# Delta-rule layer: the inverses' scratch X1 is laid into the substitution's tiles Lb and Tb

## The chip, the cores and the metric

The kernel runs on one core of one Trainium2 chip. The metric is the device time of one launch in microseconds (us), and the median over runs is compared. The engines are called as in the profile: PE (TensorE, matrix products; PEld are its weight loads), DVE (VectorE), ACT (ScalarE), POOL (GpSimd) and SP (SyncE, which issues most of the loads from DRAM). A "q" behind a name means that engine's queue of instructions.

## What is computed

A decoder trunk of four residual layers on x of 256 tokens by 1024 channels, in float32: a pooling layer, a gated delta-rule layer, a latent-attention layer, and a pooling layer again. The change lies in the delta-rule layer alone. The core of its reference:

```python
q, k, v = jnp.split(silu(causal_depthwise_conv(qkv, conv_w)), ...)
...
L = jnp.where(strict, jnp.einsum('bhnid,bhnjd->bhnij', k_beta, k) * decay, 0.0)
A = jnp.eye(C) + L
rhs = jnp.concatenate([v_beta, k_beta * jnp.exp(g)[..., None]], axis=-1)
sol = lax.linalg.triangular_solve(A, rhs, left_side=True, lower=True)
u_ps, w_cd = sol[..., :dv], sol[..., dv:]
attn = jnp.where(causal, jnp.einsum('bhnid,bhnjd->bhnij', q, k) * decay, 0.0)

def step(state, xs):            # over the chunks
    v_new = u_c - w_c @ state
    o = (q_c * exp(g_c)) @ state + a_c @ v_new
    state = state * exp(g_last) + k_dec.T @ v_new
```

There are 8 heads with keys of 128 and values of 256 channels. The triangular system is what the changed tiles serve: the kernel inverts the unit lower triangular matrices instead of solving for each right side.

## The kernel before, in words

The 256 tokens are two tiles of 128 (t = 0, 1), and the kernel takes chunks of 128 tokens, so there are 2 × 8 = 16 matrices of 128 × 128 to invert. Weights come in units of 512 KB through three buffers raw (issued by SP, L104); each is split into a rounded part whi (ACT, L117) and a remainder wlo (DVE, L119; a few on POOL), and three products of the parts stand for one float32 product (L127 to L129, and L168).

In `gdn_layer` one list sets the order of the steps on each engine's list:

```python
order = "g0 k0 d a0 g1 k1 a1 s q0 v0 v1 v2 q1 V3 i c3 g2 u0 u1 g3".split()
```

Here g are gate projections, k keys, a the lower matrices LT, s the substitution, q the queries (two halves of four heads), v values (V3 and c3 are the two halves of v3), i the inverses, u the new values. A scheduler then merges these lists, gives tiles their places in the fast memory and adds the waits. All big tiles (4 KB in each of the 128 partitions) share one pool, `s4`, which has as many slots as the program needs; a tile that takes over a slot waits until the last instruction on the slot's former tile is done.

- **Substitution (s).** The four diagonal blocks of 32 × 32 of each of the 16 matrices go from LT to DRAM (d_l) and come back as Lb, 64 partitions of one block each. POOL inverts them row by row: 31 pairs of a product pr (L728, reads Lb and Tb) and a subtraction from Tb (L732). Then Tb goes to DRAM (d_t, L735), and four transfers (L739) bring the blocks into the diagonal of the tile T. All five are on POOL's queue.
- **Queries (q1).** A projection, a short convolution (ACT L634, DVE L637 into cv), SiLU into the tile kqT (ACT, L671), then transposes (PE, L677) and products with the keys (PE, L690). POOL multiplies the last tokens' queries into Gb (L760) and works out their norms (L761 to L765); these are held back behind the substitution.
- **Inverses (i).** POOL clears a part of each scratch tile X1 (L810; the profile writes X1 and its like as X), DVE transposes T into U (L811), and two steps of doubling follow: products of LT with T (PE, L820) go masked into X1 (DVE, L822), products of X1 with U (PE, L826) correct U, and so on up to L847. L820 reads columns 0–31 and 64–95 of each head of T.
- **Gate 2 (g2).** Its result gsg (ACT, L557) is a big tile, too.

Of the kernel before, what the change touches and what calls it, by code (L numbers as in the profile page):

```python
# [16 lines left out]
P = 128  # L17
D = 1024
S = 256
NT = S // P  # L20
# [22 lines left out]
def trunk(ctx: ExitStack, tc: tile.TileContext, x, positions, norm_g, pool_w_in, pool_w_grp,  # L43
# [26 lines left out]
    def big(name, *dims, dt=F32):  # L70
        return s4.tile([P, *dims], dt, tag="s4", name=name)
# [4 lines left out]
    def workb(name, *dims):  # L76
        return wb.tile([P, *dims], F32, tag="wb", name=name)

    def small(name, *dims, bufs=2):
        return sm.tile([P, *dims], F32, tag=name, name=name, bufs=bufs)  # L80

    def bank(pool, name):
        return pool.tile([P, CW], F32, tag=name, name=name)
# [452 lines left out]
    def gdn_layer(i, j, hT):  # L536
        H = GDN_H
        M = NT * H
# [101 lines left out]


        Q, B = 4, 32
        Tb = big("Tb", B, B)[:M * Q]
        nc.gpsimd.memset(Tb, 0.0)
        nc.gpsimd.memset(Tb.rearrange("m r c -> m (r c)")[:, ::B + 1], 1.0)
        Ts = big("T", NT, H, P)
# [67 lines left out]
        def substitution():  # L714

            d_l = dram.tile([M * Q, B * B], F32, name="d_l")
            lv = d_l.rearrange("(t m d) (r c) -> t d r m c", t=NT, d=Q, r=B)
            for t in range(NT):
                for d in range(Q):
                    nc.sync.dma_start(out=lv[t, d],  # L720
                                      in_=LT[t][d * B:(d + 1) * B, :, d * B:(d + 1) * B])
            Lb = big("Lb", B, B)[:M * Q]
            nc.sync.dma_start(out=Lb, in_=d_l.rearrange("m (r c) -> m r c", r=B))
            pr = small("pr", 256, bufs=1)[:M * Q]
            for r in range(B - 1):
                n, c = B - 1 - r, r + 1
                pv = pr[:, :n * c].rearrange("m (a b) -> m a b", a=n)
                nc.gpsimd.tensor_tensor(out=pv, op=ALU.mult,  # L728
                                        in0=Lb[:, r, r + 1:, None].to_broadcast([M * Q, n, c]),
                                        in1=Tb[:, r:r + 1, :c].to_broadcast([M * Q, n, c]))  # L730
                tv = Tb[:, r + 1:, :c]
                mark["blocks"] = nc.gpsimd.tensor_tensor(out=tv, in0=tv, in1=pv,  # L732
                                                         op=ALU.subtract).ins
            d_t = dram.tile([M * Q, B * B], F32, name="d_t")
            nc.gpsimd.dma_start(out=d_t.rearrange("m (r c) -> m r c", r=B), in_=Tb)  # L735
            tv = d_t.rearrange("(m d) (r c) -> d r m c", d=Q, r=B)
            for d in range(Q):
                dd = slice(d * B, (d + 1) * B)
                nc.gpsimd.dma_start(out=Ts[dd, :, :, dd].rearrange("p t h c -> p (t h) c"),  # L739
                                    in_=tv[d])  # L740
            nc.vector.reciprocal(rki, rk)
            nc.vector.tensor_tensor(out=kds, in0=rk[:, 0, :], in1=DT[0][:, :, P - 1],
                                    op=ALU.mult)
            nc.vector.tensor_scalar(neG, eG[:, 1, :], -1.0, None, ALU.mult)
            nc.gpsimd.tensor_tensor(out=ktok, in0=ktok, op=ALU.mult,
                                    in1=kds[:, :, None].to_broadcast([P, H, P]))
# [54 lines left out]
        def inverses():  # L801

            U.extend(big("U", H, P) for _ in range(NT))
            X1 = [big("X1", H, P) for _ in range(NT)]
            for t in range(NT):
                nc.gpsimd.memset(X1[t][:, :, 32:64], 0.0)  # L810
                nc.vector.transpose(U[t].rearrange("p m c -> p (m c)"),  # L811
                                    T[t].rearrange("p m c -> p (m c)"))

            def blocks(a, x):
                return a.rearrange("p m (a b c) -> p m a b c", a=2, b=2)[:, :, :, x]

            def pairs(t):
                ps = bank(aux, "aux").rearrange("p (m a c) -> p m a c", m=H, a=2)
                for h in range(H):
                    nc.tensor.matmul(ps[:, h], lhsT=LT[t][:, h], rhs=blocks(T[t], 0)[:, h],  # L820
                                     start=True, stop=True)
                nc.vector.tensor_tensor(out=blocks(X1[t], 0), in0=ps, op=ALU.mult,  # L822
                                        in1=m32[:, None].to_broadcast([P, H, 2, 32]))
                ps = bank(aux, "aux").rearrange("p (m a c) -> p m a c", m=H, a=2)
                for h in range(H):
                    nc.tensor.matmul(ps[:96, h], lhsT=X1[t][:, h, :96], rhs=blocks(U[t], 1)[:, h],  # L826
                                     start=True, stop=True)
                u = blocks(U[t], 1)[:96]
                nc.vector.tensor_tensor(out=u, in0=u, in1=ps[:96], op=ALU.subtract)

            def whole(t):
                ps = bank(aux, "aux").rearrange("p (m c) -> p m c", m=H)
                for h in range(H):
                    nc.tensor.transpose(ps[:64, h], U[t][:64, h, :64], ident[:64, :64])
                nc.scalar.copy(T[t][:64, :, :64], ps[:64])
                ps = bank(aux, "aux").rearrange("p (m c) -> p m c", m=H)
                for h in range(H):
                    nc.tensor.matmul(ps[:, h], lhsT=LT[t][:64, h], rhs=T[t][:64, h, :64],
                                     start=True, stop=True)
                X = workb("X", H, 64)  # L840
                nc.vector.tensor_copy(X[64:], ps[64:])
                ps = bank(aux, "aux").rearrange("p (m c) -> p m c", m=H)
                for h in range(H):
                    nc.tensor.matmul(ps[:64, h], lhsT=X[64:, h], rhs=U[t][64:, h, 64:],
                                     start=True, stop=True)
                u = U[t][:64, :, 64:]
                nc.vector.tensor_tensor(out=u, in0=u, in1=ps[:64], op=ALU.subtract)  # L847

            for stage in (pairs, whole):
                for t in range(NT):  # L850
                    stage(t)

        def news(hf):
# [3 lines left out]
            for b in range(2):  # L857
# [6 lines left out]
                for c in range(2):  # L864
# [4 lines left out]
        steps = {"g": gate, "k": keys, "a": lower, "q": queries, "v": values, "u": news, "V": values_in,  # L869
                 "c": values_done}  # L870
        once = {"s": substitution, "d": decays, "i": inverses}
        for name in order:
            if name == "i":

                with later(mark["strip"], mark["dve"]):
                    inverses()
            elif name in once:
                once[name]()
            else:
                steps[name[0]](int(name[1]))  # L880
# [124 lines left out]
    def mla_layer(i, j, hT):  # L1005
# [203 lines left out]
        return layer_out(mla_w_out[j], yT, units(POOL_W // P), i)  # L1209

    layers = (pool_layer, gdn_layer, mla_layer)
    setups = [gdn_setup, mla_setup][:max(0, depth - 1)]
    first = cols_of(pool_w_in[0], POOL_W + (len(WINDOWS) - 1) * CW)
# [58 lines left out]
```

## Time and profile before

| | |
|---|---|
| median of 3 runs | 859.29 us (856.95 to 861.53) |
| profiled execution | 860.12 us, its span from first to last instruction 858.3 us |
| busy in the span | PE 836.9, DVE 594.2, ACT 490.2, POOL 155.2 us |
| mean granted clock of PE | 0.988 of full speed |
| HBM | read 137.79 MB, 162 GB/s over the span |

The kernel is bound by PE nearly everywhere. A row of the timeline reads: start (us from the span's start), duration, engine, line, operation, written tile <- read tiles, shapes, and in brackets how long the engine stood idle before it and what ended that. The delta-rule layer's substitution, second query half and inverses lie between 255 and 355 us.

### The profile page before, as it was taken

How to read it: one execution, taken by the hardware profiler on the slowest of the kernel's cores; microseconds unless marked ns; L12 is line 12 of the kernel's file. 1: busy time of each engine (PE TensorE's matmuls, PEld its weight loads, DVE VectorE, ACT ScalarE, POOL GpSimd, SP SyncE). 2: the span in 40 equal slices, each digit the busy share in tenths (PEclk: the TensorE clock that was granted, in tenths of full speed). 3: DMA queues.
4: the chain of work that ended last, by engine and by line, in shares of the span. 5: the costliest groups of instructions: out<-in, count | busy, mean ns of one | idle time of the engine just before them, and what ended most of it. 6: DMA issues, size and time to landing. Idle time of an engine off the chain costs nothing.

```text
span 858.3 us, 16132 instructions
## 1 busy us (share of the span) xinstructions
PE 836.9 (98%) x5967; PEld 778.9 (91%) x5967; DVE 594.2 (69%) x1140; ACT 490.2 (57%) x1007; POOL 155.2 (18%) x295
## 2 busy tenths in 40 slices
PE   6999999999999989999999999999999999999996
PEld 5999998988999988788979998999989989999986
DVE  4689866556988976355577659678767668867852
ACT  5566564467855744355465654566555475555642
POOL 4000000233237980022212002000000210000012
PEclk8999999999999999899999999999999999999999
DMA  6766666646655554123547676743552546556551
GB/s 196 245 190 185 179 194 198 194 138 198 193 141 168 171 149 131 66 67 106 173 139 217 198 171 172 195 127 97 172 163 82 175 148 209 182 179 196 190 201 50
DMA packets 109239, 140.42 MB, mean 164 GB/s; under 512 B 21228, under 2 KB 51112, under 8 KB 109160
## 3 DMA queue, kind: packets, MB, share of 16 engines
q1 hardware_dynamic: 106800, 137.65, 53.1%
q0 software_dynamic: 528, 1.58, 0.7%
q8 instruction: 47, 0.77, 0.4%
q10 hardware_dynamic: 1832, 0.16, 0.2%
q14 instruction: 32, 0.26, 0.1%
HBM read 137.79 MB, written 1.58 MB: 162 GB/s over the span
## 4 chain that ended last, share of the span: by engine, by line
PE 82%; POOL 7%; DVE 5%; DMA 3%; issue 2%; ACT 1%; SPq 0%; POOLq 0%; ACTq 0%; DVEq 0%
PE acc L168 33%; PE acc L128 11%; PE acc L127 11%; PE acc L129 11%; POOL Tb L732 3%; POOL pr L728 2%; PE aux L127 2%; PE aux L128 2%; PE aux L129 2%; DVE wlo L119 1%; DMA gain<-in_norm_g_dram 1%; DVE cv L637 1%; DVE h L304 1%; PE aux L861 1%; DMA Gb<-d_g 1%
## 5 line engine op out<-in xcount | busy, mean ns | idle before, releaser
L119 DVE TENSOR_TENSOR wlo<-raw,whi 128x512 fp32r<-128x512 f32 (+1 forms) x493 | 342.5, 717 | 162.6 <-ACT whi L117 155.4
L117 ACT CAST whi<-raw 128x512 fp32r<-128x512 f32 (+1 forms) x508 | 301.8, 617 | 256.7 <-PE acc L168 100.4
L127 PE MATMUL acc<-hTh,whi 128*128 128x256 f32 x832 | 234.3, 282 | 1.2 <-DVE vc L637 1.2
L128 PE MATMUL acc<-hTl,whi 128*128 128x256 f32 x832 | 235.0, 283 | 0.0
L129 PE MATMUL acc<-hTh,wlo 128*128 128x256 f32 x832 | 233.8, 281 | 0.0
L127 PEld LDWEIGHTS acc<-hTh,whi 128*128 128x128 f32 x832 | 156.9, 189 | 1.8 <-DVE vc L637 1.4
L128 PEld LDWEIGHTS acc<-hTl,whi 128*128 128x128 f32 x832 | 156.9, 189 | 0.4
L129 PEld LDWEIGHTS acc<-hTh,wlo 128*128 128x128 f32 x832 | 156.8, 189 | 0.2
L168 PE MATMUL acc<-wlo,yTh 128*128 128x256 f32 (+1 forms) x384 | 116.5, 319 | 0.0
L168 PE MATMUL acc<-whi,yTh 128*128 128x256 f32 (+1 forms) x384 | 116.4, 323 | 0.0
L168 PE MATMUL acc<-whi,yTl 128*128 128x256 f32 (+1 forms) x384 | 92.7, 322 | 0.0
L168 PEld LDWEIGHTS acc<-wlo,yTh 128*128 128x128 f32 x384 | 72.1, 188 | 5.1
L168 PEld LDWEIGHTS acc<-whi,yTh 128*128 128x128 f32 x384 | 71.7, 188 | 5.2
L168 PEld LDWEIGHTS acc<-whi,yTl 128*128 128x128 f32 x384 | 63.2, 188 | 5.5
L292 POOL TENSOR_TENSOR hg<-x,gain 128x256 f32<-128x256 f32 x18 | 14.9, 834 | 259.1 <-DVE x L354 257.4
L168 PE MATMUL acc<-wlo,hTh 128*128 128x512 f32 (+1 forms) x144 | 56.3, 396 | 0.4 <-DVE wlo L119 0.2
L168 PE MATMUL acc<-whi,hTh 128*128 128x512 f32 (+1 forms) x144 | 55.6, 394 | 0.7 <-ACT hTh L196 0.7
L168 PE MATMUL acc<-whi,hTl 128*128 128x512 f32 (+1 forms) x144 | 45.7, 389 | 0.0
L435 POOL COPY win<-u 128x4 f32<-128x4 f32 x8 | 2.8, 355 | 177.2 <-ACT u L429 177.2
L168 PEld LDWEIGHTS acc<-whi,hTh 128*128 128x128 f32 x144 | 27.5, 191 | 6.8 <-ACT hTh L196 1.7
L168 PEld LDWEIGHTS acc<-wlo,hTh 128*128 128x128 f32 x144 | 27.3, 190 | 6.8 <-DVE wlo L119 1.7
L168 PEld LDWEIGHTS acc<-whi,hTl 128*128 128x128 f32 x144 | 26.8, 190 | 5.5
(339 smaller groups left out, 1444.5 us busy)
## 6 DMA issues: line engine op xcount, KB each, us to landing
raw<-in_pool_w_in_dram SPq DMA_DIRECT2D x60, 512.0 KB, 4.5
raw<-in_gdn_w_in_dram SPq DMA_DIRECT2D x48, 512.0 KB, 3.9
raw<-in_pool_w_out_dram SPq DMA_DIRECT2D x32, 512.0 KB, 4.2
raw<-in_mla_w_in_dram SPq DMA_DIRECT2D x24, 512.0 KB, 4.6
raw<-in_mla_w_uq_dram SPq DMA_DIRECT2D x36, 256.0 KB, 3.4
raw<-in_pool_w_grp_dram SPq DMA_DIRECT2D x16, 512.0 KB, 4.1
raw<-in_gdn_w_out_dram SPq DMA_DIRECT2D x16, 512.0 KB, 3.7
raw<-in_mla_w_ukv_dram SPq DMA_DIRECT2D x32, 256.0 KB, 3.3
```

Source lines behind the costliest of these rows:

```text
L117: a = nc.scalar.copy(hi, v)
L119: b = e.tensor_tensor(out=lo, in0=v, in1=hi.bitcast(F32), op=ALU.subtract)
L127: nc.tensor.matmul(o, lhsT=lhs[0], rhs=rhs[0], start=start, stop=False)
L128: nc.tensor.matmul(o, lhsT=lhs[0], rhs=rhs[1], start=False, stop=False)
L129: return nc.tensor.matmul(o, lhsT=lhs[1], rhs=rhs[0], start=False, stop=stop)
L168: nc.tensor.matmul(o, lhsT=act(k, t * P, P)[x], rhs=parts[j][z][:, sl], start=k == first and x == z == 0, stop=k == last and x == 1)
L292: nc.gpsimd.tensor_tensor(out=self.early[t, a], in0=xs[t][:, sl], in1=self.g[:, sl], op=ALU.mult)
L304: nc.vector.scalar_tensor_tensor(out=h[:, cut:], in0=xs[t][:, sl], scalar=r[:, 0:1], in1=self.g[:, sl], op0=ALU.mult, op1=ALU.mult)
L637: nc.vector.scalar_tensor_tensor(out=o[:, d:], in0=ps[:, :S - d], scalar=tp(3 - d, c), in1=o[:, d:], op0=ALU.mult, op1=ALU.add)
L728: nc.gpsimd.tensor_tensor(out=pv, op=ALU.mult, in0=Lb[:, r, r + 1:, None].to_broadcast([M * Q, n, c]), in1=Tb[:, r:r + 1, :c].to_broadcast ...
L732: mark["blocks"] = nc.gpsimd.tensor_tensor(out=tv, in0=tv, in1=pv, op=ALU.subtract).ins
L861: nc.tensor.matmul(ps[:, c], lhsT=U[0][:, h, :], rhs=vR[h // 2][:, 0, c * DV:(c + 1) * DV], start=True, stop=True)
```

## The change

X1 is no longer a tile of its own. The substitution keeps its two tiles Lb and Tb whole (they use 64 of 128 partitions), and the inverses take them as scratch: X1[0] is Lb, X1[1] is Tb.

```diff
-        Tb = big("Tb", B, B)[:M * Q]
+        Tb_ = big("Tb", B, B)
+        Tb = Tb_[:M * Q]
+        free = []
...
-            Lb = big("Lb", B, B)[:M * Q]
+            Lb_ = big("Lb", B, B)
+            Lb = Lb_[:M * Q]
+            free.extend((Lb_, Tb_))
...
-            X1 = [big("X1", H, P) for _ in range(NT)]
+            X1 = [a.rearrange("p (h a) c -> p h (a c)", h=H) for a in free]
```

The pool has 29 slots before and after. Before, kqT of q1 took Lb's slot as soon as the substitution was done with it, and gsg of g2 took it after that; X1[0] lay in a slot that nothing had used, and X1[1] took Tb's. Now Lb and Tb keep their slots until the inverses are done with X1; kqT of q1 takes the slot that X1[0] had, and gsg takes Lb's when X1[0] is done. No other big tile is moved, and no instruction is added or removed. In the changed kernel's lists the lines stand 2 to 5 higher (L671 is L673, L728 is L732, L732 is L736, L739 is L743, L810 is L815, L820 is L825).

On ACT, at kqT of q1 (cv are the convolved queries; whi the splits between), the list before:

```order
L791 ACTIVATE vR_3807<-tp_3835,rki_2523 128x256
L634 ACTIVATE cv_3994<-acc_3843,tap_648 128x256
L117 CAST whi_4336<-raw_4329 128x512 [waits PE_49]
L671 ACTIVATE kqT_3980<-cv_3981 128x256 [waits DVE_49,Activation_49,Pool_49]
L117 CAST whi_4354<-raw_4351 128x512 [waits DMAHW0_49,PE_49]
L671 ACTIVATE kqT_3980<-cv_3982 128x256 [waits DVE_49,Activation_49]
```

And now:

```order
L795 ACTIVATE vR_3807<-tp_3835,rki_2523 128x256
L634 ACTIVATE cv_3994<-acc_3843,tap_648 128x256
L117 CAST whi_4334<-raw_4327 128x512 [waits PE_49]
L673 ACTIVATE kqT_3980<-cv_3981 128x256 [waits DVE_49,Activation_49]
L117 CAST whi_4352<-raw_4349 128x512 [waits DMAHW0_49,PE_49]
L673 ACTIVATE kqT_3980<-cv_3982 128x256 [waits DVE_49,Activation_49]
```

The order is the same; the first kqT instruction no longer waits for POOL.

On POOL, at the end of the substitution, the list before:

```order
L732 TENSOR_TENSOR Tb<-Tb,pr 64x2x30
L728 TENSOR_TENSOR pr<-Lb,Tb 64x31
L732 TENSOR_TENSOR Tb<-Tb,pr 64x31
L760 TENSOR_TENSOR Gb<-Gb,kqT 128x512
L761 TENSOR_SCALAR rq_2525<-ssq 128x2x4
L735 DMA d_t<-Tb 64x1024
L810 MEMSET X_4184 128x8x32
L659 TENSOR_TENSOR rq<-rq_2525,halves 128x2x4
L119 TENSOR_TENSOR wlo<-raw,whi 128x512
L739 DMA T<-d_t 32x16x32 x4
L764 TENSOR_TENSOR rq_2525<-rq 128x2x4
L760 TENSOR_TENSOR Gb<-Gb,kqT 128x512
```

And now:

```order
L736 TENSOR_TENSOR Tb<-Tb,pr 64x2x30
L815 MEMSET Lb 128x8x32
L732 TENSOR_TENSOR pr<-Lb,Tb 64x31
L736 TENSOR_TENSOR Tb<-Tb,pr 64x31
L764 TENSOR_TENSOR Gb<-Gb,kqT 128x512
L765 TENSOR_SCALAR rq_2525<-ssq 128x2x4
L739 DMA d_t<-Tb 64x1024
L661 TENSOR_TENSOR rq<-rq_2525,halves 128x2x4
L119 TENSOR_TENSOR wlo<-raw,whi 128x512
L743 DMA T<-d_t 32x16x32 x4
L768 TENSOR_TENSOR rq_2525<-rq 128x2x4
L815 MEMSET Tb 128x8x32
```

The memset of X1[0] (now in Lb) moved from behind d_t to ahead of the last pair of the substitution; that of X1[1] (now in Tb) moved up from behind the split wlo that follows the second Gb product, to ahead of that product. The lists of PE, DVE, ACT and SP hold the same instructions in the same order as before, with X1's name changed.

## The prediction

> **What bounds the kernel now.** I began with the page: the span, the busy times and the chain that ended last.
>
> ```profile
> span 858.3 us, 16132 instructions
> PE 836.9 (98%) x5967; PEld 778.9 (91%) x5967; DVE 594.2 (69%) x1140; ACT 490.2 (57%) x1007; POOL 155.2 (18%) x295
> PE 82%; POOL 7%; DVE 5%; DMA 3%; issue 2%; ACT 1%; SPq 0%; POOLq 0%; ACTq 0%; DVEq 0%
> ```
>
> TensorE (PE) is busy 98% of the span, so a change gains only what it takes out of PE's idle time or its slow clock. What stands out is POOL, busy 18% of the span, with 7% of the chain. The timeline around the change shows where POOL enters; I read ACT, POOL, PE and DVE there in turn.
>
> ```profile
> 301.17 0.66 ACT L117 CAST whi<-raw 128x512 fp32r<-128x512 f32 x1
> 305.29 0.42 ACT L671 ACTIVATE kqT<-cv 128x256 f32<-128x256 f32 x1 [3.46 <-POOL pr L728]
> 305.02 0.23 POOL L728 TENSOR_TENSOR pr<-Lb,Tb 64x31 f32<-64x31 f32 x1
> 303.07 0.28 PE L129 MATMUL acc<-hTh,wlo 128*128 128x256 f32 x1
> 305.76 0.69 PE L677 MATMUL tp<-ident,kqT 128*128 128x128 f32 x2 [2.41 <-ACT kqT L671]
> 306.25 1.12 DVE L119 TENSOR_TENSOR wlo<-raw,whi 128x512 fp32r<-128x512 f32 x1 [2.25 <-ACT whi L117]
> 300.14 2.80 DVE L637 SCALAR_TENSOR_TENSOR cv<-acc,tap,cv 128x254 f32<-128x254 f32 x6
> ```
>
> ACT is free at 301.83 and stands 3.46 us, until the last product that reads Lb (305.02 + 0.23) is done: the second half of the queries, kqT, lies in Lb's slot. PE, done at 303.35, stands 2.41 us for the transposes of kqT. DVE stands 2.25 us for a split queued on ACT behind kqT. The convolution that feeds kqT was not late: six steps take 2.80 us, and the first two of them complete the first tile by about 301.1.
>
> PE pays for this stall twice. The windows view, cut where the granted clock (PEclk) changes, shows it:
>
> ```profile
> core 0: us, PE busy (x) PEld busy (x) DVE busy (x) ACT busy (x) POOL busy (x), PEclk, DMA share, GB/s
> 298.49:301.90 3.41, 3.41 (x32) 3.41 (x31) 3.34 (x7) 3.34 (x9) 3.02 (x6) 1.00 0.86 224
> ...
> 301.90:305.31 3.41, 1.45 (x13) 1.25 (x11) 2.06 (x5) 0.02 (x1) 2.81 (x8) 1.00 0.40 105
> 305.31:308.72 3.41, 2.96 (x14) 2.96 (x15) 2.47 (x5) 3.12 (x7) 3.24 (x6) 0.50 0.38 136
> ```
>
> After a window in which PE was idle 1.96 of 3.41 us, the next 3.41 us ran at clock 0.50. With 2.96 us of work in it, that cost half, 1.48 us. So the stall delays PE by 2.41 + 1.48 = 3.89 us.
>
> Whether that is a delay of the kernel is decided at the next place where PE meets POOL: the inverses' first product (L820), which reads T, the tile that POOL's substitution fills through DRAM. I followed POOL there.
>
> ```profile
> 305.33 0.25 POOL L732 TENSOR_TENSOR Tb<-Tb,pr 64x31 f32<-64x31 f32 x1
> 305.54 1.27 POOL L760 TENSOR_TENSOR Gb<-Gb,kqT 128x512 f32<-128x512 f32 x1
> 306.90 0.52 POOL L761 TENSOR_SCALAR rq<-ssq 128x8 f32<-128x8 f32 x1
> 307.48 0.67 POOL L735 DMA_DIRECT2D d_t<-Tb  x1
> 308.14 0.34 POOL L810 MEMSET X<- 128x256 f32 x1
> 308.42 1.85 POOL L659 TENSOR_TENSOR rq<-rq,halves 128x8 f32<-128x8 f32 x1
> 310.25 1.27 POOL L119 TENSOR_TENSOR wlo<-raw,whi 128x512 fp32r<-128x512 f32 x1
> 311.48 1.39 POOL L739 DMA_DIRECT2D T<-d_t  x2
> 312.86 1.29 POOL L739 DMA_DIRECT2D T<-d_t  x2
> ...
> DMA to landing us min/median/max: 3.0/3.0/3.0
> ...
> T<-d_t POOLq DMA_DIRECT2D x1, 64.0 KB, 5.0
> ...
> T<-d_t POOLq DMA_DIRECT2D x1, 64.0 KB, 5.9
> ...
> SPq L104 <- POOL wlo L119: 4.1, 1, 4.1
> ```
>
> No row here has an idle bracket: POOL works without a pause from the substitution to the four transfers into T. The lines below the timeline are the times from issue to landing of d_t, of the first and of the second T transfer, and the wait of SP's queue, whose next weight load stood 4.1 us for that last POOL split. The first T transfer lands at 311.48 + 5.0 = 316.5. The second starts at about 312.2 (half of 1.39 us on) and lands at about 318.1. L820 reads columns 0–31 and 64–95 of each head, which two of the four transfers fill.
>
> ```profile
> 317.79 0.19 PEld L168 LDWEIGHTS acc<-whi,hTh 128*128 128x128 f32 x1
> 318.21 1.86 PEld L820 LDWEIGHTS aux<-T,LT 128*128 128x128 f32 x16 [0.24 <-issue]
> 318.75 1.25 DVE L811 STREAM_TRANSPOSE U<-T 128x1024 f32<-128x1024 f32 x1 [1.91 <-DMA T<-d_t]
> ```
>
> PE loads L820's weights at 318.21, 0.24 us after it was ready and 0.1 us after the second landing; DVE, which needs all four, starts at 318.75. So two paths meet at 318.1: PE's own, with the 3.89 us of stall in it, and POOL's substitution with its two trips through DRAM. The chain that ended last runs along the first; the second is at most 0.2 us shorter. This decides the forecast.
>
> **The change part by part.** *kqT's slot.* In the changed program kqT takes the slot that X1 had, which no tile used before it, and its wait on POOL is gone. ACT can begin it at 301.83, 3.46 us earlier, and PE its transposes at 303.35. What is late next? kqT's third quarter, which waits for DVE's convolution:
>
> ```profile
> 307.85 0.42 ACT L671 ACTIVATE kqT<-cv 128x256 f32<-128x256 f32 x1 [0.29 <-DVE cv L637]
> 310.09 0.27 PE L677 MATMUL tp<-ident,kqT 128*128 128x128 f32 x1
> ```
>
> DVE moves up by its 2.25 us, so this quarter is ready at 307.85 + 0.42 − 2.25 = 306.0; PE, 3.89 us earlier, asks at 306.2. It holds by 0.2 us. PE therefore reaches L820 at about 318.1 − 3.9 = 314.2.
>
> *T's landing.* Nothing in the change lets POOL start or finish the substitution sooner: its first product waits for Lb's arrival as before. One memset (0.34 us) now stands ahead of the substitution's last step and no longer behind d_t. d_t starts 0.34 us later and lands at 307.48 + 0.34 + 3.0 = 310.8, still before 311.5, where POOL has done the same rows in another order. The other memset goes ahead of a Gb product, behind the T transfers: 0.34 us for POOL's next split, which PE's rows use several us later; without that cover it would cost those 0.34 us. SP's weight loads wait for the POOL split at 310.25, so they stay beside T's transfers. What can move T is contention: DVE, which stood from 304.0 to 306.25, will work beside the substitution's tail.
>
> ```profile
> 262.35 0.33 POOL L728 TENSOR_TENSOR pr<-Lb,Tb 64x87 f32<-64x87 f32 x1
> 303.13 0.66 POOL L728 TENSOR_TENSOR pr<-Lb,Tb 64x87 f32<-64x87 f32 x1
> L119 DVE TENSOR_TENSOR wlo<-raw,whi x61: 675/693/1735, 251.6 to 399.8; 128x512 fp32r<-128x512 f32 x61
> ```
>
> The same POOL product took 0.33 us in one place and 0.66 in another; a DVE split took 0.69 in the median and up to 1.74. One more disturbed POOL step costs 0.33, three 1.0; fewer later disturbances could return 0.3. I take +0.2, nearest to a single one, with ends −0.3 and +1.0. [...]
>
> *So the saved 3.89 us become a wait.* PE stands before L820 from 314.2 to 318.3, about 4 us where it stood 0.2. ACT and DVE stand with it; DVE's transposes of T start at 318.6 + 0.2 whatever came before.
>
> *The clock.* The wait is also a new idle window, and it has a price of the kind seen above. From the other windows:
>
> ```profile
> core 0: us, PE busy (x), PEclk, DMA share, GB/s
> 349.69:353.10 3.41, 2.18 (x19) 1.00 0.45 154
> 353.10:356.51 3.41, 3.41 (x20) 0.50 0.00 0
> 356.51:359.92 3.41, 3.41 (x9) 0.50 0.00 0
> ...
> 296.18 0.39 PE L127 MATMUL acc<-hTh,whi 128*128 128x256 f32 x1 [1.15 <-DVE vc L637]
> ```
>
> PE's idle 1.15 us ahead of 296.18 cost no clock (1.00 in 298.49:301.90, further up); 1.23 us of idle in a window of small products (3.41 − 2.18) did, for two windows. Four us of idle fill more than half of at least one window of 3.41 us, however the windows lie. A whole slow window after 318.3 costs 3.41 × 0.5 = 1.7 us; if the slow clock sets in while PE still stands, as little as 0.7. PE's timeline has no idle bracket from there to 350, so this passes on. I take 1.4, between the two and nearer to the whole window that the stall at 303 had.
>
> *Nothing else.* Order and waits elsewhere are unchanged; gsg, which takes over Lb's slot, also loses a wait on POOL, with no time in it.
>
> **The sum**, against the profiled execution (860.12, of which span 858.3): −3.9 stall and its slow clock, +3.9 wait for T (less the 0.1 to 0.2 that PE waited already), +0.2 for T, +1.4 slow clock = +1.6, so 861.7. That execution lies 0.83 over the median of the three runs shown, 859.29; on the median it gives 860.9.
>
> **The rivals.** *B: the wait costs no clock.* PE stands before L820 and goes on at full speed: +0.2, 859.5. Against it stands 301.90:305.31, where less idle was enough. [...]
>
> *C: T comes sooner, and the gain survives.* T's transfers take 5.0 to 5.9 us beside two weight loads, d_t 3.0 with none. If ACT's and DVE's lead moved the loads out of the way, T could land up to 2.4 to 2.9 us sooner, and the time would be 855.4 (all 3.89 us gained) to 856.9 (2.4). Against it: the loads wait for a POOL split that stands still in time.
>
> *D: slower, by two slow windows.* L820 is made of short products (64 columns). If they count as little as those at 353.10, the clock stays at 0.50 for 6.82 us: up to 3.4, at least 0.7 + 1.7 = 2.4; I take 3.1. With T at +0.2 that is 859.29 + 3.3 = 862.6. It decides for slower by over 0.5% once T lands another 1.0 us late.
>
> **How the numbers follow.** A, the stall moves and one slow window follows: 0.55, 860.9 (its own range 859.7 to 862.0, from −0.3 + 0.7 to +1.0 + 1.7). B: 0.17. C: 0.08. D: 0.20. The shown runs spread from 856.95 to 861.53, so 0.5%, 4.3 us, is about what a measurement of this kernel can tell from no change. Faster means below 855.0, slower above 863.6. Faster comes only from C's lower half with some scatter: 0.05. Slower comes from half of D and a little of A: 0.11. The rest, 0.84, is the same. The range takes in A, B and most of D, and leaves out half of C and D's upper end: 857.0 to 864.0.
>
> **What would show it.** In the changed kernel: no POOL bracket at kqT and none at PE's transposes of it; clock 1.00 where it was 0.50 after 305.3; a wait of 3 to 4 us on T before L820 (L825 there), on PE or its weight loads; T's second landing within 1 us of 318.1; a window at 0.50 shortly after. If T lands at 316 or before, C holds and I am wrong. If PE does not wait before L820, the third quarter of kqT or another wait has taken the lead away. If the clock stays at 1.00 there, B holds.

## The result, and the profile after

The changed kernel takes 863.96 us (median of 11 runs, 860.57 to 866.53) where the kernel before, on the same chip, takes 860.85 us (11 runs, 856.95 to 862.35). The ratio is 1.0045, with a 95% interval of 1.0028 to 1.0061: slower by 3 to 4 us (the medians differ by 3.1, the ratio gives 3.9). The forecast, 860.9, was no measurable change; its range reached to 864.0.

The page of the changed kernel's profiled execution (866.53 us, the longest of the 11 runs, so what it shows is larger than usual):

```profile
span 864.8 us, 16131 instructions
PE 839.3 (97%) x5967; PEld 781.3 (90%) x5967; DVE 591.4 (68%) x1140; ACT 489.3 (57%) x1007; POOL 156.9 (18%) x295
PE 83%; POOL 7%; DVE 4%; DMA 2%; issue 2%; ACT 1%; SPq 1%; POOLq 0%; ACTq 0%; DVEq 0%
```

Busy times and chain shares are those of before within a percent or so, so they tell nothing here; the stage around the change does. Its timeline, ACT and PE first, then POOL and DVE:

```profile
301.78 0.47 ACT L673 ACTIVATE kqT<-cv 128x256 f32<-128x256 f32 x1
305.23 0.42 ACT L673 ACTIVATE kqT<-cv 128x256 f32<-128x256 f32 x1 [0.61 <-DVE cv L637]
...
314.09 0.40 PE L168 MATMUL acc<-whi,hTh 128*128 128x512 f32 x1
321.19 3.64 PE L825 MATMUL aux<-T,LT 128*128 128x64 f32 x16 [6.70 <-DMA T<-d_t]
...
308.89 0.58 POOL L736 TENSOR_TENSOR Tb<-Tb,pr 64x31 f32<-64x31 f32 x1
311.07 0.67 POOL L739 DMA_DIRECT2D d_t<-Tb  x1
314.63 2.67 POOL L743 DMA_DIRECT2D T<-d_t  x4
...
321.55 2.37 DVE L816 STREAM_TRANSPOSE U<-T 128x1024 f32<-128x1024 f32 x2 [9.52 <-DMA T<-d_t]
```

kqT waits for POOL no more. PE, without the stall, is done at 314.49 and then stands 6.70 us for T. The substitution ends 3.9 us later than before (309.47 against 305.58): 1.24 us of that is a later start, 2.65 its length, 47.28 us against 44.63. The windows, cut where the granted clock changes:

```profile
core 0: us, PE busy (x) PEld busy (x) DVE busy (x) ACT busy (x) POOL busy (x), PEclk, DMA share, GB/s
311.75:315.17 3.42, 2.74 (x12) 1.88 (x10) 0.27 (x2) 0.00 (x0) 3.41 (x3) 1.00 0.36 77
315.17:318.58 3.41, 0.00 (x0) 0.00 (x0) 0.00 (x0) 0.00 (x0) 3.39 (x7) 1.00 0.73 214
318.58:321.99 3.41, 0.80 (x4) 0.83 (x5) 0.44 (x1) 2.48 (x5) 3.24 (x5) 0.50 0.70 180
321.99:325.41 3.42, 3.42 (x16) 3.32 (x16) 3.42 (x6) 0.00 (x0) 0.98 (x3) 0.50 0.43 148
325.41:328.82 3.41, 3.41 (x9) 2.64 (x9) 3.41 (x8) 0.00 (x0) 0.00 (x0) 0.50 0.48 131
```

Three windows follow at 0.50, with 0.80 + 3.42 + 3.41 = 7.63 us of PE work in them, so at half the clock I put the loss at 3.8 us (L825's 16 products took 3.64 us there, the same 16 in the kernel before 1.96). The kernel before has the full clock from the same product (its L820) on:

```profile
core 0: us, PE busy (x), PEclk, DMA share, GB/s
318.25:321.66 3.41, 3.41 (x24) 1.00 0.53 157
```

Wait and clock together are 10.5 us, where the stall and its slow window were 3.89: 6.6 us more, and the two spans differ by 6.5.

Two questions follow. Why does T come later? And is the change bad by itself, or only because T is late?

### The profile page after: what moved, and what is told of

The parts are those of the page before. It is cut to its first block, busy times and chain, and to the rows that moved or that the text cites. A ratio compares the mean times of both kernels' runs of the same rounds, so it can differ in the third digit from the quotient of the medians.

```text
span 864.8 us, 16131 instructions
## 1 busy us (share of the span) xinstructions
PE 839.3 (97%) x5967; PEld 781.3 (90%) x5967; DVE 591.4 (68%) x1140; ACT 489.3 (57%) x1007; POOL 156.9 (18%) x295
## 4 chain that ended last, share of the span: by engine, by line
PE 83%; POOL 7%; DVE 4%; DMA 2%; issue 2%; ACT 1%; SPq 1%; POOLq 0%; ACTq 0%; DVEq 0%
PE acc L168 34%; PE acc L128 11%; PE acc L129 11%; PE acc L127 11%; POOL pr L732 3%; POOL Tb L736 2%; PE aux L127 2%; PE aux L128 2%; PE aux L129 2%; DVE wlo L119 1%; DMA x<-in_x_dram 1%; PE aux L866 1%; DMA T<-d_t 1%; DVE h L304 1%; PE aux L825 1%
```

## The experiments

Theory 1: nothing in the change costs but the loss of the stall. While ACT stood at kqT, DVE stood too and left POOL alone; now DVE's weight subtractions run beside the substitution's tail and hold its steps up, and PE waits longer for T, with more slow clock behind it. Rivals: the first profile was a chance; or the scratch's new place costs by itself. Line numbers of an experiment shift by a few.

**Both kernels again.** No edit; a second profile of each, from one run each.

> The changed kernel once more, for a second profile. Theory 1 (the substitution's tail on POOL now runs beside the weight subtractions of DVE, which the old stall kept away, and each of them holds a POOL step up): the substitution takes 46.5 to 48 us again (47.3 in the first profile, 44.6 before the change), the second transfer of T lands 2 to 3.5 us later than before the change, PE idles 5.5 to 7.5 us ahead of L825 and two or three clock windows there are at 0.50. Rival (the first profile was a chance late one): the substitution takes 44.6 within 0.5, T lands within 1 us of 318.1, and PE idles about 4 us.

> The kernel before once more, for a second profile. Theory 1: the substitution takes 44.6 us within 0.8 and has 24 of the weight subtractions beside it, within one; kqT waits 3 to 4 us for POOL; PE reaches the first product of the inverses about when T lands, and waits under 0.5 us there. Rival (the length of the substitution varies from run to run by some us): 46 us or more in this one.

Measured: 864.2 and 859.16 us. After: substitution 47.1 us, PE idle 6.90 us ahead of L825, three windows at 0.50 (315.89 to 326.13). Before: 44.8 us, stall 2.38 us, no wait for T. As theory 1 has it, but for T's second landing: at 319.21 it is 1.1 us later than in the first profile of the kernel before and 1.9 later than in its second (317.27), where 2 to 3.5 were expected. What holds the steps up can be read where the two engines' rows lie beside each other. The tail of the changed kernel, POOL and DVE:

```profile
303.22 0.80 POOL L732 TENSOR_TENSOR pr<-Lb,Tb 64x135 f32<-64x135 f32 x1
305.14 0.37 POOL L732 TENSOR_TENSOR pr<-Lb,Tb 64x112 f32<-64x112 f32 x1
305.59 0.82 POOL L736 TENSOR_TENSOR Tb<-Tb,pr 64x112 f32<-64x112 f32 x1
308.19 0.62 POOL L732 TENSOR_TENSOR pr<-Lb,Tb 64x31 f32<-64x31 f32 x1
...
303.07 0.68 DVE L119 TENSOR_TENSOR wlo<-raw,whi 128x512 fp32r<-128x512 f32 x1
304.66 0.87 DVE L637 SCALAR_TENSOR_TENSOR cv<-acc,tap,cv 128x253 f32<-128x253 f32 x2
305.44 0.68 DVE L119 TENSOR_TENSOR wlo<-raw,whi 128x512 fp32r<-128x512 f32 x1
...
308.03 1.33 DVE L119 TENSOR_TENSOR wlo<-raw,whi 128x512 fp32r<-128x512 f32 x2 [0.40 <-ACT whi L117]
```

The same steps in the kernel before:

```profile
301.17 0.41 POOL L728 TENSOR_TENSOR pr<-Lb,Tb 64x135 f32<-64x135 f32 x1
...
302.19 0.37 POOL L728 TENSOR_TENSOR pr<-Lb,Tb 64x112 f32<-64x112 f32 x1
302.64 0.42 POOL L732 TENSOR_TENSOR Tb<-Tb,pr 64x112 f32<-64x112 f32 x1
305.02 0.23 POOL L728 TENSOR_TENSOR pr<-Lb,Tb 64x31 f32<-64x31 f32 x1
```

The three steps that lie under a subtraction (two operands from SBUF) take 0.4 us more; the step under a convolution step (305.14; one operand from PSUM) takes 0.37 us in both kernels. The source view, over the substitution alone, counts the subtractions. The kernel before:

```profile
L119 DVE TENSOR_TENSOR wlo<-raw,whi x24: 675/962/1137, 263.3 to 302.9; 128x512 fp32r<-128x512 f32 x24
```

The changed kernel:

```profile
L119 DVE TENSOR_TENSOR wlo<-raw,whi x29: 675/812/1139, 261.9 to 308.6; 128x512 fp32r<-128x512 f32 x29
```

Five more of them, 2.65 us: 0.53 us each. (The columns behind the count are the shortest, median and longest in ns.) The subtractions themselves are stretched from 0.68 to 1.1 us, so both engines pay.

**Another instruction in the subtractions' place**, in both kernels, from q0 to V3 (the condition that limits it to these steps isn't shown). It leaves out the low halves of these weights:

```diff
-b = e.tensor_tensor(out=lo, in0=v, in1=hi.bitcast(F32), op=ALU.subtract)
+b = e.tensor_reduce(lo, hi.bitcast(F32).rearrange("p (c o) -> p c o", o=1),
+                    axis=AX.X, op=ALU.add)     # reads hi alone
```

> The changed kernel with another instruction in the place of DVE's weight subtractions while the substitution runs (the projections q0 to V3): a reduction over one element, which reads whi alone, 128x512 as before, and writes wlo. The low halves of those weights are left out (wlo is a copy of whi). Theory 1 (a DVE instruction with two operands from SBUF and a POOL step exclude each other, one with a single operand does not): a POOL step is 0.23 to 0.6 us long by its size throughout, the substitution takes 34 to 38 us in place of 47, T lands 9 to 12 us earlier, PE doesn't wait ahead of the inverses, no clock window at 0.50 lies there: 853 to 857 us. Rival (the steps are long for another reason, as the DMA traffic or PE's): the substitution stays at 46 us or more, and the time at 862 to 865.

> The kernel before with the same reduction in the place of the subtractions, the low halves of those weights left out in the same way. Theory 1: the substitution is over 8 us or so before kqT would need its place, so the stall at kqT is gone here too; with neither wait left the change has nothing to move: this and the run above within 0.2% of each other, 853 to 857 us. Rival: kqT still waits 2 us or more for POOL, and this one is slower than the one above by 2 us or more, or the change costs as in the old pair, and this one is 3 us faster.

Measured: 852.07 and 852.53 us; ratios to the kernel before 0.9897 (0.9879 to 0.9915) and 0.9910 (0.9889 to 0.9932), both a little under the 853 to 857 us expected. The tile view of the first, pr and Tb in the substitution, and the source view of the new instruction there:

```profile
L737 POOL TENSOR_TENSOR pr<-Lb,Tb x31: 232/511/631, 260.0 to 296.9; 64x31 f32<-64x31 f32 x2, 64x60 f32<-64x60 f32 x2, 64x87 f32<-64x87 f32 x2, 64x112 f32<-64x112 f32 x2
L741 POOL TENSOR_TENSOR Tb<-Tb,pr x31: 247/599/771, 260.3 to 297.4; 64x31 f32<-64x31 f32 x2, 64x60 f32<-64x60 f32 x2, 64x87 f32<-64x87 f32 x2, 64x112 f32<-64x112 f32 x2
...
L121 DVE TENSOR_REDUCE wlo<-whi x21: 672/676/689, 262.0 to 290.7; 128x512 fp32r<-128x512 f32 x21
```

No step is over 0.77 us now, and the DVE instruction keeps its 0.68 us. The substitution takes 37.6 us (38.1 in the other), and its last transfer lands at 309.6, ahead of PE's arrival at 310.67. In the other kernel one step is longer, 1.29 us where it takes 0.23 alone; it lies beside two plain subtractions of the next unit (1.28 us), which follow those of V3. So the collisions cost 6.6 us in the kernel before (44.6 against 38.1) and 9.6 in the first profile of the changed one (47.3 against 37.6). Set beside the same steps in these two runs, 24 of the 62 POOL steps are longer in the kernel before, with its 24 subtractions, and 28 in the changed one, with its 29: about one step for each subtraction, most of them by 0.33 us. With neither stall nor wait left, the two kernels are 0.05% apart: the scratch's new place costs nothing that four runs of each can show (their intervals reach 0.2% to either side). (The edit also moves some of PE's rows around the second query half, alike in both, so the gain against the kernel before is not the collisions' alone.)

**The same two operands in another form**, in the same steps, one run and then twelve:

```diff
-b = e.tensor_tensor(out=lo, in0=v, in1=hi.bitcast(F32), op=ALU.subtract)
+b = e.scalar_tensor_tensor(out=lo, in0=v, scalar=1.0, in1=hi.bitcast(F32),
+                           op0=ALU.mult, op1=ALU.subtract)
```

> The changed kernel with DVE's weight subtractions in another form in the same stretch: scalar_tensor_tensor (raw times 1 less whi), which still reads two operands from SBUF, with the same order on every engine. Theory 1 (it is the two operands from SBUF that exclude POOL): nothing changes, substitution 46 to 48 us, 862 to 866 us. [...]

> The changed kernel with scalar_tensor_tensor for the weight subtractions beside the substitution once more, timed: its one run took 857.93 us, under all 12 of the changed kernel, with a substitution of 45.3 us (26 subtractions beside it), T at 316.4, a wait of 2.46 us ahead of the inverses' first product and no clock window at 0.50 behind it. Theory 1 (the same two operands from SBUF, so the form is nothing, and the run was one in which the subtractions fell luckily): the times spread from 858 to 866 us, ratio 1.001 to 1.006. Rival (the form does shift when the subtractions fall, so that fewer lie beside the substitution): ratio 0.996 to 0.999, the wait under 3 us.

> The kernel before with the same form. Theory 1: nothing changes, since PE comes to the inverses after T in any case: ratio 0.998 to 1.002. Rival (the form shortens the substitution by 2 us): kqT is freed 2 us sooner, ratio 0.996 to 0.998.

Measured: 857.93 us in the first run, which missed my figure by 4 us. Twelve more runs gave 862.74 us, 1.0039 (1.0025 to 1.0053), and the kernel before with this form 859.33, 0.9996 (0.9981 to 1.0010). So the form is nothing, and the first run was luck, 3.2 us under the lowest of the twelve (861.16). PE's timeline and a window show what luck is here. The first run:

```profile
316.56 1.97 PE L829 MATMUL aux<-T,LT 128*128 128x64 f32 x16 [2.46 <-DMA T<-d_t]
...
core 0: us, PE busy (x) PEld busy (x) DVE busy (x) ACT busy (x) POOL busy (x), PEclk, DMA share, GB/s
316.56:320.00 3.44, 3.44 (x23) 3.18 (x24) 2.93 (x4) 0.62 (x1) 1.78 (x3) 1.00 0.52 157
```

The profile taken with the twelve:

```profile
317.73 1.51 PE L829 MATMUL aux<-T,LT 128*128 128x64 f32 x6 [4.81 <-DMA T<-d_t]
```

In the first the substitution ran 45.3 us with 26 subtractions beside it and began 3 us sooner than in the first profile of the changed kernel; a wait of 2.46 us followed, no window at 0.50, and L825's 16 products took 1.97 us, where they took 3.64 at the slow clock. The later profile has 45.6 us, a wait of 4.81 and three windows. Half of the difference between the two waits comes from PE, which was at L825 at 314.1 in the first and at 312.9 in the later one.

**The old wait put back**, everything else of the change kept:

```diff
+nc.gpsimd.memset(zero, 0.0)            # behind the substitution's last step
...
-nc.scalar.activation(dst[hf][:, 2 * b + c, :], cv[c], AF.Silu)
+nc.scalar.activation(dst[hf][:, 2 * b + c, :], cv[c], AF.Silu, bias=zero)   # q1 only
```

> The changed kernel with the old wait alone put back: the four activations that write the second half of the queries (kqT) take their zero bias from a small tile that POOL sets behind the last step of the substitution. The inverses' scratch still lies in Lb and Tb. Theory 1 (the change costs only because the wait is gone: DVE then runs on beside the substitution's tail, T comes later, and PE waits for it longer): kqT waits 3 to 4 us for POOL, the substitution takes 44.6 us within 0.8, T lands about 318, PE waits under 1 us ahead of the inverses' first product, and the time is that of the kernel before, ratio 0.998 to 1.002. Rival (the new place of the scratch costs by itself): the stall comes on top, 1.004 to 1.009.

Measured: 860.08 us, ratio 1.0005 (0.9989 to 1.0022): the kernel before's time. The stall was longer than I wrote, the rest as expected (substitution 45.4 us, no wait for T):

```profile
305.76 0.51 ACT L675 ACTIVATE kqT<-cv,zero 128x256 f32<-128x256 f32 x1 [5.94 <-POOL zero L743]
306.32 0.69 PE L683 MATMUL tp<-ident,kqT 128*128 128x128 f32 x2 [4.86 <-ACT kqT L675]
```

A stall added to the changed kernel makes it faster by 3 to 4 us (ratio 1.0005 where it was 1.0045). So the lost wait is the cause, and all else in the change is worth less than the interval, some 0.2%.

**The inverses later**, in both kernels:

```diff
-"... q1 V3 i c3 g2 u0 u1 g3"
+"... q1 V3 g2 i c3 u0 u1 g3"
```

> The changed kernel with the inverses written after the third gate (order V3 g2 i c3 in place of V3 i c3 g2): PE runs 35 more products of 512 columns (35 x 0.233 = 8.2 us) before the first product that needs T. Theory 1 with a clock loss: the 6.7 us wait for T and the about 3.8 us of slow clock after it both go, since PE would come to L825 at 314.5 + 8.2 = 322.7 and T lands at 321: 853.5 to 858 us, unless the end of the inverses becomes late for u0. Rival (the wait for T is only where the work behind it shows its own lateness, the chain through U decides): the wait comes back ahead of u0 or the heads, 862 to 866 us.

> The kernel before with the same new order, so that the pair with the run above differs by the change alone. Theory 1: the stall at kqT stays (2.4 us idle and 1.5 us of slow clock), no wait for T was there to be won: 858 to 861.5 us, and the changed kernel of this pair is 3 to 5 us faster than this one, where in the old order it was 3.9 us slower. Rival (the change costs by itself, for instance through what lies beside what in SBUF): the changed kernel is slower in this order too, by 2 to 5 us.

Measured: 860.18 us, 0.9998 (0.9981 to 1.0015), and 862.03 us, 1.0020 (1.0003 to 1.0037). With 35 more products ahead of it, L825 waits for nothing, and the changed kernel is 1.85 us below the other where it lost 3.1. The two intervals overlap, so a gain isn't shown, only that the loss is gone. The distance is under the 3 to 5 us that I expected, and both times are over their figures, 860.18 by 2 us and 862.03 by 0.5. PE's timeline and the windows of the changed kernel in this order show the wait gone, and where most of the missing part went:

```profile
322.15 1.89 PE L825 MATMUL aux<-T,LT 128*128 128x64 f32 x16
```

```profile
345.81:359.46 13.65, 12.09 (x64) 10.71 (x65) 2.10 (x4) 1.42 (x3) 0.00 (x0) 0.50 0.10 37
```

The same stage of the changed kernel in its own order:

```profile
359.54:366.37 6.83, 6.83 (x28) 5.72 (x28) 0.68 (x1) 1.68 (x4) 0.00 (x0) 0.50 0.01 2
```

The stage of small products at the inverses' end, two windows at 0.50 in that (6.83 us of PE work), now has four (12.09 us). My reading, which no run tests by itself: gate 2's long products, which stood between the small ones (351.01 to 354.24 in the changed kernel's own order), have been used up ahead of them. The two windows more return 12.09/2 − 6.83/2 = 2.6 us. The kernel before has four such windows in this order, too (349.54 to 363.19).

**T on SyncE's queue**, first its four transfers, then also d_t, in both kernels:

```diff
-nc.gpsimd.dma_start(out=Ts[dd, ...], in_=tv[d])
+nc.sync.dma_start(out=Ts[dd, ...], in_=tv[d])
```

> The changed kernel with the four transfers of T issued by SyncE's queue in place of POOL's. Issues of SyncE take 0.05 to 0.4 us where POOL's take 0.65 to 0.74, and transfers of 32 KB land 2.4 us after an issue of SyncE, where T's land 4.6 to 5.7 us after one of POOL's: T should land about 317 instead of 321. With T expected sooner the order puts the inverses' first product ahead of the 13 products of 512 columns (3.0 us), so that PE comes to it at about 311.5: a wait of 5 to 6 us remains, with two or three clock windows. Theory 1 (T's landing against PE's arrival decides): 859.5 to 862.5 us. Rival (T's time is not what counts, the later stages make it up): 863 to 866 us.

> The kernel before with T's transfers on SyncE's queue. The stall at kqT stays (3.9 us with its slow clock); T lands about 313.5 and PE comes to the first product, which now stands ahead of the 13 products, at about 315.2: no wait, and the inverses start 3 us sooner. Theory 1: 858 to 860.5 us, faster than the run above by 1 to 3 us. Rival (the stall at kqT costs and T's wait doesn't): slower than the run above.

> The changed kernel with both trips of the substitution's result on SyncE's queue, d_t as well as the four transfers of T: d_t is issued as soon as the last step is done and no longer behind the Gb product (1.3 to 1.5 us). T should land about 2 us sooner than with T's transfers alone on that queue, some 1 us after PE comes to the first product. Theory 1 (the change gains what the stall at kqT cost as soon as T is there in time): wait under 1.5 us, at most one clock window, 854 to 857.5 us, and faster than the next run by 0 to 3 us. Rival (what the change takes away at kqT always comes back): slower than the next run by 2 us or more. Part of the first layer's loads stand in another order in both runs of this pair, so they are compared with each other first.

> The kernel before with both trips on SyncE's queue, the same order on every engine as in the run above, but kqT still in Lb's slot. Theory 1: T lands 3 us or more before PE comes to the first product, the stall at kqT stays with 2.4 us of idle time and 0 to 3 us of slow clock: 856 to 859 us, slower than the run above by 0 to 3 us. Rival: faster than the run above by 2 us or more.

Measured: 861.05 us, 1.0015 (1.0002 to 1.0029), and 857.07 us, 0.9969 (0.9951 to 0.9987); then 856.94 us, 0.9977 (0.9960 to 0.9993), and 857.30 us, 0.9976 (0.9959 to 0.9993). The tile view of T gives the times from issue to landing, first in the kernel before, then in it with T's transfers on SyncE's queue:

```profile
DMA to landing us min/median/max: 5.0/5.4/5.9
```

```profile
DMA to landing us min/median/max: 2.1/2.1/2.1
```

3.3 us less per transfer. (SyncE's issues of T took 0.33 to 0.49 us each, not 0.05 to 0.4 as I had written.) In the four runs the places where PE waits for POOL read, in the order of the texts above (the changed kernel and the kernel before with T's transfers moved, then both again with d_t moved too):

```profile
314.56 3.24 PE L825 MATMUL aux<-T,LT 128*128 128x64 f32 x16 [3.22 <-DMA T<-d_t]
```

```profile
304.88 0.44 PE L677 MATMUL tp<-ident,kqT 128*128 128x128 f32 x2 [2.38 <-ACT kqT L671]
```

```profile
313.42 3.65 PE L825 MATMUL aux<-T,LT 128*128 128x64 f32 x16 [3.54 <-DMA T<-d_t]
```

```profile
304.35 0.44 PE L677 MATMUL tp<-ident,kqT 128*128 128x128 f32 x2 [3.05 <-ACT kqT L671]
```

With T's transfers alone moved, the change still cost 4.0 us. The direction is theory 1's, the size over its 1 to 3: the scheduler also sets the first product earlier, PE waits 3.22 us (5 to 6 expected), and two windows at 0.50 follow. With d_t moved too, wait (3.54) and old stall (3.05) are alike, and the times are 0.4 us apart. That is a balance in these profiles: behind the wait stand two windows at 0.50 (2.8 us lost) and behind the stall none, while the kernel before has two in the stage of small products (3.4 us) and the changed one none. That PE would wait under 1.5 us, with at most one slow window, was wrong: it came 1.5 us sooner than with T's transfers alone (309.9 against 311.3). The kernel before with T's transfers on SyncE's queue beats both kernels of this case (857.07 us). PE had no wait for T there to lose. What its profile lacks is slow clock: none of the three windows at 0.50 that the kernel before has in this layer, worth 1.48 + 3.41 = 4.9 us, where the spans differ by 4.1. Why they are gone isn't shown.

## Why the prediction was wrong

- *kqT and PE's way to L825*: right. No wait on POOL; PE came at 314.49, forecast 314.2 (312.4 to 314.1 in the profiles after it). kqT's third quarter did not stop PE.
- *The stall comes back as a wait for T*: right in kind, and shown: put the stall back and the time is that of before (1.0005); take both away and the change is worth nothing (852.07 and 852.53).
- *The clock, 1.4 us*: the step that failed. I allowed for one window. In the old order the changed kernel's four profiles (two of them with the other form of the subtraction) have waits of 6.70, 6.90, 4.81 and 2.46 us, and three, three, three and no windows at 0.50 behind them; the losses to the clock are 3.8, 3.4, 4.0 and 0, in the mean 2.8, twice the term. With the waits that is 8.0 us in the mean. The three of the kernel before have 3.1 us of stall and 1.6 of slow clock: 4.7. So PE saves 4.7 us, waits 5.2, which is near the forecast's −3.9 and +3.9, and pays 2.8 on top. The difference, 3.3 us, is the measured 3 to 4.
- *The same, read from the spans*: L825 starts at 318.7 in the mean of the four and at 318.3 in the mean of the three, so all that stall and T can do comes to 0.4 us, where +0.2 was forecast. From L825's start to the end of the span the four take 543.6, 543.1, 543.9 and 539.7 us, and the three 540.1, 539.5 and 538.4. Of the 3.7 us by which the mean spans differ, 3.3 lie there, and they go with the slow windows behind the wait: the profile without them, 539.7, is like those of before. The profile with the stall put back fits, too. It loses 7.8 us at its stall (4.86 and 3.0 of slow clock), comes to L825 only at 320.0, and takes 539.5 from there. PE came to that stall 1.9 us sooner than in the kernel before, so the losses of a single profile don't add up to its time.
- *T's landing, +0.2 with +1.0 as the upper end*: too low for the first profile, where the second transfer lands 2.9 us later (321.05 against 318.11); in the mean of the same profiles it lands at 318.6 against 317.8, 0.75 us later and inside the ends. The term allowed for one more disturbed POOL step, 0.33 us. But DVE stays ahead for the whole tail, and the weights of the next unit follow. Over the seven profiles in which kqT was held back the substitution took 44.6 to 45.4 us, mean 45.0, with 24 or 25 subtractions; over the seven in which it was not, 45.3 to 47.3, mean 46.2, with 26 to 29 (those with the reduction left out). So the substitution is 1.2 us longer, where my row gave 0.33. Part of this is made up before T lands (in the first profile d_t follows the last step by 1.60 us, in the kernel before by 1.90).
- *The rivals*: B fell (one profile of four has no slow clock, and then a shorter wait). C fell: T landed sooner than 317 in one profile only, at 316.43, still after C's 316, and there the substitution had begun sooner. D, with 0.20, came nearest: slow clock through L825's short products, +3.3 us with two windows at 3.1. Measured are 3.1 to 3.9, from three windows in three profiles of four. That it is the shortness of these products that keeps the clock down isn't shown: in the fourth profile the same 16 ran at 1.00 and took 1.97 us. The rows at 353.10 that D rests on were worth more than I gave them.
- *The chances*: the shown spread of 4.6 us hid that eleven runs of each can tell 0.45% from nothing.

What stays open: why the substitution's start varies by 3 us from run to run, which is as much as the change is worth. Dummy work on PE during the wait, which would price the clock apart from the wait, wasn't tried; the clock's share is read from the traces alone.

## What to carry to other kernels

A wait that is removed ahead of a meeting of two engines buys nothing while the other engine is late, and can cost: the freed engines may slow the late one (here DVE's subtractions lengthened most of POOL's disturbed steps by 0.33 us), and one long wait can lose more clock than a short one (here 3.8 us behind a wait of 6.70, 1.48 behind one of 2.41). Before taking a stall away, ask what else stood still in it and whom that helped. Here the late side is where time lies: with the collisions gone both kernels are 1% faster, though with the low halves of some weights left out. Four small transfers on another queue gave the kernel before 0.3%, by a way that isn't shown.

## What the runs showed of the hardware

Where the granted clock fell behind a wait of PE in these profiles, it was 0.50 for whole windows of 3.41 us (three from 318.58 to 328.82 in the changed kernel). A wait of 2.38 us (the kernel before with T's transfers on SyncE's queue), one of 2.46 (the first run with the other form) and one of 3.05 (the kernel before with both trips on SyncE's queue) had no such window behind them; 2.41 (the kernel before) had one; 3.22 and 3.54 (the changed kernel in the runs with SyncE's queue) had two, 4.81 (the changed kernel with the other form, the later profile) three, 4.86 (the old wait put back) two, 6.70 and 6.90 (the changed kernel) three. Outside the stage of small products the least that had one is 2.05 us, ahead of 277.66 in the first run with the other form (278.19:281.60 is at 0.50); 1.11 us at that place in the kernel before had none (277.89:281.30 is at 1.00). The window that was idle throughout (315.17:318.58) still shows 1.00, the next one 0.50; and 325.41:328.82 is at 0.50 though PE was busy in all of the window before it. Each of these waits of 3.2 us and more had a slow window behind it, while the one of 3.05 had none and the one of 2.41 already cost one.

A DVE instruction of 128x512 with two operands from SBUF and a POOL step of 64 partitions slowed each other here: 24 steps beside 24 subtractions in the kernel before, 28 beside 29 in the changed one, most of them by 0.33 us, and the subtractions took up to 1.1 us in place of 0.68. The other form of the instruction did the same in its first run (25 steps beside 26, up to 1.13 us). Beside the one with a single operand from SBUF (the reduction, in the changed kernel) no step took over 0.77 us.
